# Reordering the projections, the key copies and the exponentials of a hybrid attention/recurrence layer

## The chip, the core and the metric

The program runs on one core of one Trainium2 chip. The metric is the device time of one execution, in microseconds (us): lower is better. Names of engines below: PE is the matrix engine (matmuls and transposes), PEld its weight loads, DVE the vector engine, ACT the scalar engine, POOL the general engine, and SP the queue from which all transfers of this kernel are issued. Each of them has its own list of instructions, written in the order of the source; semaphores hold an instruction until what it needs is there, and what stands behind it on its list waits too.

## What is computed

One decoder layer over 1024 tokens of width 1024, in float32. After an RMSNorm, one projection feeds two mixers: dilated sliding-window attention with 8 heads of 64, and a gated linear recurrence (HGRN2) with 4 heads of 128. Their outputs are joined and projected, and a squared-ReLU MLP of width 4096 follows. The part that matters here, cut down from the reference:

```python
q_a, k_a, v_a, q_h, f_h, i_h, g_h = jnp.split(h @ w_in[layer], splits, axis=-1)
for window, dilation in ((128, 1), (512, 4), (2048, 16)):
    s = einsum(q, k) * 64 ** -0.5 + alibi_bias          # causal, keys by stride
    m = max(s);  p = exp(s - m);  den = sum(p);  o = p @ v / den
attn = sum_i softmax_i(m_i + log den_i) * o_i           # three patterns joined per position
rec  = hgrn2_recurrence(q_h, f_h, i_h, g_h, ...)
x = x + rmsnorm(concat[rmsnorm(attn), rec] @ w_out)
x = x + rmsnorm(relu(rmsnorm(x) @ w_ff1) ** 2 @ w_ff2)
```

## The kernel before

**Split numbers.** Each float32 matrix is kept as two halves, a rounded high part and the remainder. `split_into` makes them: ACT copies the high part (L85), DVE subtracts it (L86). A projection is a chain of `three_pass` steps of three matmuls (L89, L90, L91), high by high, low by high, high by low.

**Stages.** The recurrence heads come first, one after the other (`hgrn_core`). While one runs, PE is kept busy with the projections of the next. In the last of them (h = 3) the projections of the attention pairs 0 and 1 begin. Then comes the attention loop of 64 steps; the out-projection and the MLP follow, and the change does not touch their code.

**The attention loop.** Eight heads in four pairs. A head has eight steps, `ITEMS`: D0 to D3 (the first four blocks of queries, densely), F0 and F1 (far keys, four classes of stride), N0 and N1 (near keys of the last four blocks). Step s is item s % 8 of head s // 8, and a pair takes 16 steps. Inside a step these helpers are called, and their order in the source is the order on each engine:

- `raise_` takes the exponentials of the *next* step's scores on ACT (L883; a D item has one, F and N items have two), which need the negative row maximum in `stat`. For F and N that maximum is joined over the patterns by `joint` (L869, L870 on DVE), from a small matmul `px` (`swap_max`, L864).
- `look` makes scores for a later step: matmuls with the key halves `kh` and `kl` into a bank `ps` (L828, L829), then bias and maximum on DVE (L833).
- `turn` transposes this step's exponentials on PE (`pt_D` L893, `pt_N` L902, `pt_F` L905), then copies the high half on ACT (L915, L917, L922) and subtracts on DVE (L918, L920, L923).
- `weigh` multiplies a turned item by the values, one step later (`pov`, `pov_far`; L939, L951, L957). `finish` turns the result back (L977), adds on DVE (L981) and divides on POOL (L982).
- `fill` takes projection steps from a list of generators, `queue`, and puts them between these. A unit is one `three_pass`, three matmuls. `UNITS` says how many units a step gets, half ahead of `weigh` and half at the end of the step; steps without an entry ask for a time instead (`fill(500.0)`).

**The projections of a pair** (`attn_proj`, six half projections of eight units). Queries, both halves (`pm_aq`); then values, both halves (`pm_av`); then keys, both halves (`pm_ak`). A half of the values is scaled on DVE (L746, tile `vf`), transposed on PE (`pvt`, L729), copied on ACT (L732) and subtracted on DVE (L733). A half of the keys is read from its bank on DVE (L677, tile `kf`), copied into `kh` twice on ACT (L688, 64 partitions each), subtracted into `kl` twice on POOL (L689), and four transfers bring each half to the other 64 partitions (L692, L693). The second half of the keys goes on a list, `put_off`, and `keys_late` does all of its work at once: in step 13 of a pair's 16 steps, after `while not put_off: fill(1.0)` has put the rest of the key projection on PE in one go. Step 14 then makes the first scores of the next pair from these keys. Pair `pr + 2` enters the queue in step 14 of pair `pr`.

**The last pair.** Heads 6 and 7 have no projections of attention left beside them. PE is filled with the recurrent half of the out-projection of the first four row blocks (`early_out`, tile `pwe`, 32 units). Its left operands are the rows `erows`, multiplied by a gain on POOL (`row_rec`, L1026), turned on PE (`pmt`, L1066) and split on ACT and DVE into `emt`. The table `hooks` names the steps in which these and the splits of the weights (`w_get`, tiles `wh`, `wl`, `woh`, `wol`) are done.

Of the kernel before, what the change touches and what calls it, by code (L numbers as in the profile page):

```python
# [17 lines left out]
P = 128  # L18
# [19 lines left out]
def hymba_layer(ctx, tc, x, w_in, w_out, w_ff1, w_ff2, g_pre, lb_logits, g_mix, g_post,  # L38
# [414 lines left out]
    def hgrn_core(h, scale, after=None):  # L453
# [128 lines left out]
        if h == HH - 1:  # L582
            while not put_off:
                fill(1.0)
            keys_late()
# [21 lines left out]
        fill(1500 * scale)  # L607
        for n in range(NT):
            V.scalar_tensor_tensor(gate[:, n], pos[n // 4][:, n % 4], rs[:, n:n + 1], gate[:, n],
                                   op0=ALU.mult, op1=ALU.mult)  # L610
# [61 lines left out]
    put_off = []  # L672

    def keys_read(pr, pm, hf):
# [4 lines left out]
        return full  # L679

    def keys_off(pr, stacks, full, hf):

        def place_of(t):
            return t.rearrange("p (r m) -> p r m", r=DIL)[:, :, hf * P:(hf + 1) * P]
        src = full.rearrange("p (r m) -> p r m", r=DIL)
        for i, (a, b) in enumerate(halves):
            kh, kl = (place_of(stacks[i][n])[a:b] for n in ("kh", "kl"))
            S.activation(kh, src[a:b], AF.Copy)  # L688
            G.tensor_tensor(out=kl, in0=src[a:b], in1=f32(kh), op=ALU.subtract)  # L689
        for n in ("kh", "kl"):  # L690
            k0, k1 = (place_of(f32(stacks[i][n])) for i in range(2))
            nc.sync.dma_start(out=k0[64:128], in_=k0[0:64])  # L692
            nc.sync.dma_start(out=k1[0:64], in_=k1[64:128])  # L693

    def keys_late():
        while put_off:
            pr, stacks, src, hf, read = put_off.pop()
            keys_off(pr, stacks, src if read else keys_read(pr, src, hf), hf)

    def attn_proj(pr):  # L700
        stacks = [{}, {}]
        box = [None]
        w = w_get(A0 + 3 * pr, 0)
        for hf in range(2):
            sl = slice(hf * 512, hf * 512 + 512)
            for n, cost in enumerate(proj_t(w, f"aq{pr}", hf, box)):
                if hf == 0 and n == 4:
                    w_get(A0 + 3 * pr)
                yield cost
# [12 lines left out]
        w = w_get(A0 + 3 * pr + 1, 0)  # L722
        vs = slab("V8", f"v{pr}", F32R, (P, NT, 2, 2, 64))
        late = None

        def v_turn(full, hf):
            pt = bank("mm", f"pvt{pr}{hf}")
            for j in range(4):
                TE.transpose(pt[:, j * P:(j + 1) * P], full[:, j * P:(j + 1) * P], ident)  # L729
            ptv = pt.rearrange("p (j h d) -> p j h d", j=4, h=2)  # L730
            dst = vs[:, hf * 4:hf * 4 + 4]
            S.activation(dst[:, :, :, 0, :], ptv, AF.Copy)  # L732
            V.tensor_tensor(out=dst[:, :, :, 1, :], in0=ptv, in1=f32(dst[:, :, :, 0, :]), op=ALU.subtract)  # L733
        for hf in range(2):
            sl = slice(hf * 512, hf * 512 + 512)
            n = 0
            for cost in proj_t(w, f"av{pr}", hf, box):
                n += 1
                if n == 4 and late is not None:
                    v_turn(*late)  # L740
                    cost += 450.0
                if n == 5 and hf == 0:
                    w_get(A0 + 3 * pr + 1)
                yield cost
            full = half(f"vf{pr}{hf}")
            V.tensor_tensor(out=by_class(full), in0=in_blocks(box[0]), in1=in_blocks(rrow[:, sl]), op=ALU.mult)  # L746
            late = (full, hf)
            yield 650.0
        while pr > 0 and not first_done[pr - 1]:
            yield None  # L750
        w = w_get(A0 + 3 * pr + 2, 0)
        for i in range(2):
            stacks[i]["kh"] = slab("S", f"kh{pr}_{i}", F32R)
            stacks[i]["kl"] = slab("S", f"kl{pr}_{i}", F32R)
        for hf in range(2):
            sl = slice(hf * 512, hf * 512 + 512)
            n = 0
            for cost in proj_t(w, f"ak{pr}", hf, box):
                n += 1
                if n == 3 and hf == 0:  # L760
                    v_turn(*late)
                    cost += 450.0
                if n == 6 and hf == 0:
                    for r in range(DIL):
                        nc.sync.dma_start(out=v_dram[pr][r].rearrange("(n i) c -> i n c", i=32),
                                          in_=f32(vs[32 * r:32 * r + 32]).rearrange("p n h a d -> p n (h a d)"))
                    if pr == 0:
                        far_load(0)
                if n == 6 and hf == 0:
                    w_get(A0 + 3 * pr + 2)  # L770
                yield cost
            if hf == 0 and pr == AH // 2 - 1:
                early_rows()
            if hf == 0:
                keys_off(pr, stacks, keys_read(pr, box[0], hf), hf)
            else:
                put_off.append((pr, stacks, box[0], hf, False))
            pairs[pr] = (stacks, vs)
            yield 650.0

# [91 lines left out]
    def raise_(hd, kind, g):  # L872
# [9 lines left out]
        for pe, i in jobs:  # L882
# [305 lines left out]
    def open_attention():  # L1188
# [3 lines left out]
        look(0, "N", 0)  # L1192

    for h in range(HH):
# [9 lines left out]
        43: lambda: row_rec(0),  # L1204
        44: lambda: w_get(WO0, 0),
        45: lambda: [drain(), row_turn(0, 0, tag="mm"), w_get(WO0 + 1, 0), row_rec(1)],
# [984 lines left out]
```

## Time and profile before

| | before |
|---|---|
| median of 3 runs | 1235.7 us (1234.51 to 1236.78) |
| the profiled execution: time / span of its profile | 1235.14 us / 1233.0 us |
| PE busy | 1209.1 us, 98% of the span |
| DVE / ACT / POOL busy | 862.0 / 546.4 / 322.4 us |
| mean granted PE clock over the span | 0.993 |
| transfers | 174.21 MB, mean 141 GB/s |

The span runs from the first to the last instruction; 2.1 us of the profiled time lie outside it. Busy time of PE includes matmuls that overlap their neighbours' ends, so 98% says that PE had something in hand, not that it ran at its best. The granted clock is the share of full speed that PE was given. A trace has each instruction's start and length and, in square brackets, how long its engine sat idle before it and what ended that. The recurrence ends at about 302 us, the attention loop runs from there to about 540 us, and the rest is the out-projection and the MLP.

### The profile page before, as it was taken

How to read it: one execution, taken by the hardware profiler on the slowest of the kernel's cores; microseconds unless marked ns; L12 is line 12 of the kernel's file. 1: busy time of each engine (PE TensorE's matmuls, PEld its weight loads, DVE VectorE, ACT ScalarE, POOL GpSimd, SP SyncE). 2: the span in 40 equal slices, each digit the busy share in tenths (PEclk: the TensorE clock that was granted, in tenths of full speed). 3: DMA queues.
4: the chain of work that ended last, by engine and by line, in shares of the span. 5: the costliest groups of instructions: out<-in, count | busy, mean ns of one | idle time of the engine just before them, and what ended most of it. 6: DMA issues, size and time to landing. Idle time of an engine off the chain costs nothing.

```text
span 1233.0 us, 17255 instructions
## 1 busy us (share of the span) xinstructions
PE 1209.1 (98%) x6350; PEld 1032.7 (84%) x6350; DVE 862.0 (70%) x1478; ACT 546.4 (44%) x1067; POOL 322.4 (26%) x321
## 2 busy tenths in 40 slices
PE   9999999999999999999999999999999999999998
PEld 8898989888878787878888888888888888888886
DVE  5697979786656556758679666576669655388796
ACT  7633324223555556666565222222235353434462
POOL 0110101012112123146150676756632000000022
PEclk9999999999999998999999999999999999999999
DMA  5231413125252527354333546455487634433337
GB/s 215 69 91 56 120 56 107 35 80 149 64 132 81 140 72 185 95 191 137 115 137 126 190 170 231 173 186 179 143 308 283 239 98 159 154 98 91 120 101 274
DMA packets 86483, 174.21 MB, mean 141 GB/s; under 512 B 12160, under 2 KB 38784, under 8 KB 86400
## 3 DMA queue, kind: packets, MB, share of 16 engines
q1 hardware_dynamic: 86400, 173.12, 43.2%
q8 instruction: 50, 0.82, 0.3%
q14 instruction: 33, 0.27, 0.1%
HBM read 117.76 MB, written 49.04 MB: 135 GB/s over the span
## 4 chain that ended last, share of the span: by engine, by line
PE 90%; ACT 3%; DVE 3%; issue 1%; DMA 1%; SPq 0%; POOL 0%; DVEq 0%; POOLq 0%; ACTq 0%
PE f L1931 18%; PE f2s L1931 7%; PE pig L91 2%; PE pig L89 2%; PE pig L90 2%; PE pl L480 2%; PE pwo L90 2%; PE pwo L91 2%; PE pwo L89 2%; PE pm_av L89 1%; PE pm_f L89 1%; PE pm_f L91 1%; PE pm_av L91 1%; PE pm_f L90 1%; PE pm_av L90 1%
## 5 line engine op out<-in xcount | busy, mean ns | idle before, releaser
L86 DVE TENSOR_TENSOR al<-ar,ah 128x1024 fp32r<-128x1024 f32 x56 | 70.6, 1261 | 80.2 <-ACT ah L85 77.8
L1931 PE MATMUL f<-bh,ah 128*128 128x512 f32 x320 | 124.5, 389 | 0.0
L1931 PE MATMUL f<-bl,ah 128*128 128x512 f32 x320 | 124.5, 389 | 0.0
L1931 PE MATMUL f<-bh,al 128*128 128x512 f32 x320 | 124.5, 389 | 0.0
L85 ACT ACTIVATE ah<-ar 128x1024 fp32r<-128x1024 f32 x56 | 59.2, 1057 | 90.1 <-DMA ar<-actd 85.9
L1931 PEld LDWEIGHTS f<-bh,ah 128*128 128x128 f32 x320 | 60.1, 188 | 12.6
L1931 PEld LDWEIGHTS f<-bl,ah 128*128 128x128 f32 x320 | 60.1, 188 | 12.5
L1931 PEld LDWEIGHTS f<-bh,al 128*128 128x128 f32 x320 | 60.1, 188 | 12.4
L2005 POOL TENSOR_SCALAR lbl<-ssq 128x1 f32<-128x1 f32 x4 | 3.3, 821 | 244.3 <-ACT fd L2001 244.2
L1554 POOL TENSOR_TENSOR e<-x,e 128x512 f32<-128x512 f32 x14 | 21.6, 1540 | 132.4 <-DVE x L1505 132.4
L1931 PE MATMUL f2s<-bh,al 128*128 128x512 f32 (+1 forms) x128 | 48.9, 382 | 0.0
L1931 PE MATMUL f2s<-bl,ah 128*128 128x512 f32 (+1 forms) x128 | 48.9, 382 | 0.0
L1931 PE MATMUL f2s<-bh,ah 128*128 128x512 f32 (+1 forms) x128 | 48.9, 382 | 0.0
L982 POOL TENSOR_TENSOR anat<-anat,stat 128x128 f32<-128x128 f32 (+1 forms) x24 | 13.1, 544 | 124.8 <-DVE anat L981 120.7
L86 DVE TENSOR_TENSOR bl<-br,bh 128x1024 fp32r<-128x1024 f32 x32 | 40.1, 1253 | 0.9 <-ACT bh L85 0.8
L664 POOL COPY tout<-traw 128x256 f32<-128x256 f32 x16 | 11.8, 736 | 107.3 <-DMA traw<-in_bias_tab_dram 73.7
L1948 ACT ACTIVATE acc<-f 128x512 f32<-128x512 f32 x28 | 16.8, 598 | 45.9 <-PE f L1931 45.8
L86 DVE TENSOR_TENSOR wl<-raw,wh 128x1024 fp32r<-128x1024 f32 x23 | 29.1, 1267 | 10.3 <-ACT wh L85 10.2
L85 ACT ACTIVATE bh<-br 128x1024 fp32r<-128x1024 f32 x32 | 33.6, 1050 | 3.9 <-PE f L1931 2.8
L689 POOL TENSOR_TENSOR kl<-kf,kh 64x512 fp32r<-64x512 f32 x16 | 20.5, 1279 | 47.7 <-ACT kh L688 47.1
L89 PE MATMUL pwo<-woh,mt 128*128 128x512 f32 x80 | 31.7, 397 | 0.5 <-ACT esum L1089 0.5
L718 POOL TENSOR_TENSOR ql<-qf,q 64x512 fp32r<-64x512 f32 x16 | 21.4, 1336 | 40.3 <-ACT q L717 28.5
(1702 smaller groups left out, 4029.3 us busy)
## 6 DMA issues: line engine op xcount, KB each, us to landing
ar<-actd SPq DMA_DIRECT2D x56, 512.0 KB, 3.7
br<-in_w_ff_dram SPq DMA_DIRECT2D x16, 1024.0 KB, 6.1
w1r<-in_w_ff_dram SPq DMA_DIRECT2D x14, 1024.0 KB, 6.5
raw<-in_w_in_dram SPq DMA_DIRECT2D x26, 512.0 KB, 3.8
actd<-e SPq DMA_DIRECT2D x17, 768.0 KB, 4.2
actd<-e SPq DMA_DIRECT2D x11, 1024.0 KB, 4.1
vd<-v SPq DMA_DIRECT2D x16, 256.0 KB, 3.8
raw<-in_w_out_dram SPq DMA_DIRECT2D x8, 512.0 KB, 4.2
```

Source lines behind the costliest of these rows:

```text
L85: S.activation(hi, src, AF.Copy)
L86: eng.tensor_tensor(out=lo, in0=src, in1=f32(hi), op=ALU.subtract)
L89: TE.matmul(dst, lhs[0], rhs[0], start=start, stop=False)
L90: TE.matmul(dst, lhs[0], rhs[1], start=False, stop=False)
L91: TE.matmul(dst, lhs[1], rhs[0], start=False, stop=stop)
L480: TE.matmul(pl[:, n % 2, :192], kt[:, n * P:(n + 1) * P], sets[u // 2][:, n % 4], start=True, stop=True)
L689: G.tensor_tensor(out=kl, in0=src[a:b], in1=f32(kh), op=ALU.subtract)
L718: G.tensor_tensor(out=lo[a:b], in0=full[a:b], in1=f32(stacks[i]["q"][a:b, sl]), op=ALU.subtract)
L982: G.tensor_tensor(out=dst, in0=dst, in1=st["rd"][:, b].unsqueeze(2).to_broadcast([P, n, 64]), op=ALU.mult)
L1554: eng[0].tensor_tensor(out=e1[:, 3], in0=a21, in1=e1[:, 2], op=ALU.add)
L1931: TE.matmul(pm, a[:, j, c], b[:, j, d], start=start and j == 0 and q == 0, stop=stop and j == 1 and q == 2, skip_group_check=True)
L1948: S.activation(acc_at(p, i), pm, AF.Copy)
```

## The change

Six things are done together; the arithmetic and the number of instructions of each kind stay.

1. A pair projects its queries, then the first half of its values, then both halves of its keys, then the second half of its values. The turning of a half of the values (`values_turn`) is taken out of its fixed place and done in a later projection.
2. The key work is cut into four jobs for each pair (one for each head of the pair and each half): one ACT copy, one POOL subtraction, two transfers. `key_job` does one job per step, in steps 1, 2, 3, 6 and 7 of a head. (Pair 0 does its jobs at once.)
3. Of the two exponentials of an F or N item the second stands behind `turn` in the step, not ahead of it.
4. `joint` for the near items comes one step earlier (4, not 5); `far_queries` comes earlier in its step; the first near scores of head 0 stand behind one more fill.
5. All four pairs stand in the queue from the start; a pair waits for `second_done` of the pair two before it. `UNITS` has four rows, and every step of the loop is filled by it.
6. `hooks` does the preparation of the early out-projection one to two steps later: the first row's gain in step 45 (43 before), the first row turn in 47 (45), the second in 50 (49), the third in 52 (51).

```diff
@@ hgrn_core
         if h == HH - 1:
-            while not put_off:
+            while keys_done[0] < 2:
                 fill(1.0)
-            keys_late()
...
         fill(1500 * scale)
+        if h == HH - 1:
+            look(0, "N", 0)
@@ keys
+        key_jobs.extend((pr, i, hf, full) for i in range(2))
+        keys_done[pr] += 1
...
+    def key_job():
+        if not key_jobs:
+            return
+        pr, i, hf, full = key_jobs.pop(0)
+        a, b = halves[i]
...
+        S.activation(kh[a:b], src, AF.Copy)
+        G.tensor_tensor(out=kl[a:b], in0=src, in1=f32(kh[a:b]), op=ALU.subtract)
+        c, d = halves[1 - i]
+        for t in (kh, kl):
+            nc.sync.dma_start(out=f32(t[c:d]), in_=f32(t[a:b]))
+
+    def values_turn():
+        pr, vs, full, hf = turn_later.pop(0)
+        pt = bank("mm", f"pvt{pr}{hf}")
...
@@ attn_proj
+        while pr > 1 and not second_done[pr - 2]:
+            yield None
...
+                if hf == 0 and n == 2 and turn_later:
+                    values_turn()
...
+        def values(hf):
+            for n, cost in enumerate(proj_t(wv, f"av{pr}", hf, box)):
+                if n == 4:
+                    w_get(A0 + 3 * pr + 1 + hf)
+                yield cost
...
+        yield from values(0)
         while pr > 0 and not first_done[pr - 1]:
             yield None
...
+            keys_read(pr, box[0], hf)
             if hf == 0 and pr == AH // 2 - 1:
                 early_rows()
...
+        yield from values(1)
@@ the loop
-    UNITS = ((2, 3, 4, 3, 2, 2, 2, 2), (3, 3, 4, 4, 3, 2, 2, 2), (4, 4, 4, 4, 3, 3, 3, 3))
+    UNITS = ((2, 3, 3, 4, 3, 3, 3, 3), (3, 3, 3, 4, 2, 3, 3, 2), (3, 3, 3, 4, 2, 3, 3, 2), (2,) * 8)
...
+    queue += [attn_proj(2), attn_proj(3)]
...
-        if i in (3, 5):
-            joint(hd, int(i == 5))
-        raise_(*((hd, *ITEMS[i + 1]) if i < 7 else (hd + 1, *ITEMS[0])))
-        if s % 16 == 13 and s < n_steps - 16:
-            while not put_off:
+        if i in (3, 4):
+            joint(hd, int(i == 4))
+        coming = (hd, *ITEMS[i + 1]) if i < 7 else (hd + 1, *ITEMS[0])
+        raise_(*coming, which=(0,))
+        if s % 16 in (11, 13) and s < n_steps - 16:
+            while keys_done[s // 16 + 1] < (1 if s % 16 == 11 else 2):
                 fill(1.0)
...
         turn(hd, kind, g)
+        raise_(*coming, which=(1,))
...
-        if s % 16 == 13 and s < n_steps - 16:
-            keys_late()
+        if i in (1, 2, 3, 6, 7):
+            key_job()
+        if s == 47:
+            drain()
+            values_turn()
+            early_sums()
+            queue.extend(early_out(t) for t in range(NE))
```

**What moves on PE at the border from pair 0 to pair 1** (last items of head 1, first scores of head 2). In a name such as `pt1_F1` the first digit is the head; in `pm_ak11` the digits are the pair and the half; the number behind the last underscore is a buffer. Line numbers of the changed kernel are a few higher. Before:

```order
L91 MATMUL pm_ak11_3607<-hTh11_94,wl21_3297 128x512
L905 MATMUL pt1_F1_3662<-ident_77,pf1_3378 128x128 x3
L951 MATMUL pov1_far_3672<-ptFh1_3619,vf0_0_2949 128x128
...
L977 MATMUL pov1_1_3633<-ident_77,pd1_3377 128x128 x2
L828 MATMUL ps2_D0_3701<-kh1_0_3494,q1_0_3140 128x128
L829 MATMUL ps2_D0_3701<-kl1_0_3495,q1_0_3140 128x128
L902 MATMUL pt1_N0_3706<-ident_77,pn1_3436 128x128 x4
```

Now, with the units of the next pair's queries and the turned values of this pair between them:

```order
L91 MATMUL pm_aq20_3659<-hTh00_88,wl22_3615 128x512
L908 MATMUL pt1_F1_3664<-ident_77,pf1_3394 128x128 x3
L89 MATMUL pm_aq20_3659<-hTh00_88,wh22_3614 128x512
...
L980 MATMUL pov1_1_3644<-ident_77,pd1_3393 128x128 x2
...
L710 MATMUL pvt11_3693<-ident_77,vf11_3657 128x128 x4
...
L831 MATMUL ps2_D0_3713<-kh1_0_3341,q1_0_3132 128x128
L832 MATMUL ps2_D0_3713<-kl1_0_3342,q1_0_3132 128x128
L905 MATMUL pt1_N0_3718<-ident_77,pn1_3459 128x128 x4
```

Between the turn of F1 and the turn of N0 there stood no unit of projection; now three units and a turn of values stand there. Five units of keys (15 matmuls in a row) stood right ahead of the turn of F1 before; the last key matmul now stands 44 rows ahead of it.

**What moves on ACT at the same place.** Before, the two exponentials of N0 (`pn1`, x2), the turned copies of F1, the two key copies, and the two exponentials of N1 follow one another:

```order
L883 ACTIVATE pn1_3436,stat1_3376<-pn1_3436,stat1_3376 128x256 x2
L915 ACTIVATE ptFh1_3619<-pt1_F1_3662 128x256
L917 ACTIVATE ptFh1_3619<-pt1_F1_3662 64x128 x2
L688 ACTIVATE kh1_0_3494<-kf11_3684 64x4x128
L688 ACTIVATE kh1_1_3496<-kf11_3684 64x4x128
L883 ACTIVATE pn1_3436,stat1_3376<-pn1_3436,stat1_3376 128x256 x2
L922 ACTIVATE ptNh1_3707<-pt1_N0_3706 128x4x128
```

Now:

```order
L886 ACTIVATE pn1_3459,stat1_3392<-pn1_3459,stat1_3392 128x256
L918 ACTIVATE ptFh1_3629<-pt1_F1_3664 128x256
L920 ACTIVATE ptFh1_3629<-pt1_F1_3664 64x128 x2
L886 ACTIVATE pn1_3459,stat1_3392<-pn1_3459,stat1_3392 128x256
L713 ACTIVATE v1_3262<-pvt11_3693 128x8x64
L886 ACTIVATE pn1_3459,stat1_3392<-pn1_3459,stat1_3392 128x256
L925 ACTIVATE ptNh1_3719<-pt1_N0_3718 128x4x128
L886 ACTIVATE pn1_3459,stat1_3392<-pn1_3459,stat1_3392 128x256
```

The key copies are gone from this place (the last of them stands seven rows ahead of the first exponential shown), a copy of turned values has come, and each item's second exponential stands behind the copies of the item before it.

**What moves on DVE in head 6**, in the last pair. `swap6_1` and `stat6` are the steps of `spread_max` and `joint`, `ptl6_2` the low halves of D2 and D3, `emt` the split of an early row. Before:

```order
L923 TENSOR_TENSOR ptl6_2_5194<-pt6_D2_5192,pth6_2_5193 128x3x128
L856 TENSOR_TENSOR swap6_1_5210<-stat6_5024,pick321_134 128x4x32
L869 TENSOR_TENSOR stat6_5024<-px6_0_5182,stat6_5024 128x4
L870 TENSOR_SCALAR stat6_5024<-stat6_5024 128x4
L923 TENSOR_TENSOR ptl6_2_5194<-pt6_D3_5221,pth6_2_5193 128x4x128
```

Now:

```order
L926 TENSOR_TENSOR ptl6_2_5178<-pt6_D2_5176,pth6_2_5177 128x3x128
L859 TENSOR_TENSOR swap6_1_5193<-stat6_4994,pick321_134 128x4x32
L86 TENSOR_TENSOR emt0_4778<-pmt1_0_5195,emt0_4778 128x512
L872 TENSOR_TENSOR stat6_4994<-px6_0_5166,stat6_4994 128x4
L873 TENSOR_SCALAR stat6_4994<-stat6_4994 128x4
L926 TENSOR_TENSOR ptl6_2_5178<-pt6_D3_5206,pth6_2_5177 128x4x128
```

The split of the second early row has come to stand ahead of the joined maximum, which the exponentials of F0 wait for.

More of the change, by code (lines that the diff above doesn't have):

```diff
@@ L881, in raise_ @@
             jobs = [(st["F"][:, r], 8 + r) for r in range(2 * g, 2 * g + 2)]
-        for pe, i in jobs:
+        for pe, i in (jobs[w] for w in which if w < len(jobs)):
             S.activation(pe, pe, AF.Exp, bias=st["nm"][:, i:i + 1], accum_out=st["dn"][:, i:i + 1])
@@ L1281, in hymba_layer @@
             look(hd + 1, "N", 0)
-        if s == 53:
+        if s == 54:
             row_turn(3, 0, tag="s")
```

136 lines of the change are left out of this document (50 added, 86 removed).

## The prediction

> **What bounds the kernel now.** I read the page first, then the busy time by stage, then PE's timeline where the stages lose time, then ACT and DVE at the same places.
>
> ```profile
> span 1233.0 us, 17255 instructions
> PE 1209.1 (98%) x6350; PEld 1032.7 (84%) x6350; DVE 862.0 (70%) x1478; ACT 546.4 (44%) x1067; POOL 322.4 (26%) x321
> ```
>
> PE bounds the whole; 23.9 us of its span are idle. The change adds and removes no matmul, so it can only win idle time, and time in which PE runs below its clock. The stages show where that is. Columns: window, its length, busy time (and count) of PE, PEld, DVE, ACT, POOL, then PE's granted clock.
>
> ```profile
> 296.00:544.00 248.00, 233.01 (x1369) 199.41 (x1368) 153.03 (x483) 148.79 (x396) 60.45 (x70) 0.97 0.41 110
> 300.00:304.00 4.00, 2.81 (x23) 2.54 (x22) 3.19 (x6) 0.65 (x2) 0.70 (x2) 1.00 0.60 140
> 352.00:364.00 12.00, 8.94 (x43) 7.03 (x42) 5.35 (x18) 6.37 (x20) 2.93 (x3) 0.86 0.42 97
> 416.00:428.00 12.00, 9.16 (x45) 7.51 (x44) 6.80 (x22) 5.75 (x15) 2.92 (x3) 0.86 0.45 115
> 476.00:488.00 12.00, 9.54 (x46) 8.12 (x45) 7.25 (x17) 8.53 (x22) 6.35 (x5) 0.72 0.52 124
> 492.00:504.00 12.00, 9.11 (x63) 7.89 (x62) 9.24 (x28) 8.22 (x24) 3.57 (x4) 1.00 0.72 215
> 524.00:544.00 20.00, 17.81 (x96) 13.77 (x95) 11.44 (x21) 14.98 (x42) 7.28 (x16) 1.00 0.36 98
> ```
>
> The attention loop holds 14.99 us of the idle time (248 less 233.01), and six stretches hold 14.63 of it: 1.19 at its start, 3.06, 2.84 and 2.46 at the three borders between pairs, 2.89 and 2.19 in the last pair. Only the borders also lose clock: 0.14 × 12 = 1.7 us twice and 0.28 × 12 = 3.4 us, 6.7 at most; some of it falls on idle time, so I count 6.0. The most there is to win is about 14.6 + 6 = 20.6 us.
>
> What PE waits for at the three borders, in brackets:
>
> ```profile
> 354.21 0.33 PE L951 MATMUL pov_far<-ptFl,vf 128*128 128x128 f32 x1 [0.59 <-DVE ptFl L918]
> 358.36 0.93 PE L902 MATMUL pt_N<-ident,pn 128*128 128x128 f32 x4 [2.12 <-ACT pn L883]
> ...
> 420.77 1.18 PE L902 MATMUL pt_N<-ident,pn 128*128 128x128 f32 x4 [2.12 <-ACT pn L883]
> ...
> 477.75 0.66 PE L1066 MATMUL pmt<-ident,erows 128*128 128x128 f32 x4 [1.21 <-POOL erows L1026]
> 479.17 0.45 PE L828 MATMUL ps_D<-kh,q 128*128 128x128 f32 x1 [0.76 <-DMA kh<-kh]
> 482.62 0.79 PE L89 MATMUL pwe<-wh,emt 128*128 128x512 f32 x1 [0.41 <-ACT emt L85]
> ```
>
> Why the exponentials are late at the first border, on DVE and then on ACT:
>
> ```profile
> 355.29 1.08 DVE L677 TENSOR_TENSOR kf<-pm_ak,rrow 128x512 f32<-128x512 f32 x1
> ...
> 356.40 1.28 ACT L688 ACTIVATE kh<-kf 64x512 fp32r<-64x512 f32 x2 [2.70 <-DVE kf L677]
> 357.70 0.51 ACT L883 ACTIVATE pn<-pn,stat 128x256 f32<-128x256 f32 x1
> ```
>
> The late half of the keys stands in the way: its reading (1.08), then its two copies (1.28), then the exponentials PE waits for. Nothing of the next pair could run on PE meanwhile, since the border's units had been spent ahead of it.
>
> **The change part by part.**
>
> *The borders.* Keys come before the second values, so their four jobs end two steps ahead of the border, one per step; the 1.08 + 1.28 leave the chain, and 3 units and a turn of values stand between the turns of F1 and N0 where none stood. From start to start a small product takes 0.12 us and a projection matmul 0.23, so a unit of three takes 0.7:
>
> ```profile
> 346.65 0.28 PE L939 MATMUL pov<-ptl,v 128*128 128x256 f32 x1
> 346.77 0.28 PE L939 MATMUL pov<-pth,v 128*128 128x256 f32 x1
> ...
> 447.21 0.48 PE L89 MATMUL pm_av<-hTh,wh 128*128 128x512 f32 x1
> 447.52 0.39 PE L90 MATMUL pm_av<-hTl,wh 128*128 128x512 f32 x1
> 447.75 0.39 PE L91 MATMUL pm_av<-hTh,wl 128*128 128x512 f32 x1
> ```
>
> From the turn of F1 to that of N0 PE now has three units (2.1), six far products (0.7), and ten more small ones (a finish, a turn of values, scores, 1.0), 3.8 us. ACT needs for N0 its first exponential (0.5), the copies of F1 (0.9) and the second exponential (0.5), 1.9 us. Late next is the split of the next queries' weights, now made in the second values' fifth unit and not in the keys:
>
> ```profile
> 352.89 0.36 ACT L915 ACTIVATE ptFh<-pt_F 128x256 fp32r<-128x256 f32 x1
> 353.15 0.55 ACT L917 ACTIVATE ptFh<-pt_F 64x128 fp32r<-64x128 f32 x2
> ...
> L86 DVE TENSOR_TENSOR wl<-raw,wh 128x1024 fp32r<-128x1024 f32 x23 | 29.1, 1267 | 10.3 <-ACT wh L85 10.2
> L85 ACT ACTIVATE bh<-br 128x1024 fp32r<-128x1024 f32 x32 | 33.6, 1050 | 3.9 <-PE f L1931 2.8
> ```
>
> About 3.6 us of PE lie ahead of its first use, against 1.05 (the copy, priced by one of the same shape) and 1.27, 2.3 us; if a second piece of that size is queued in front, it costs 0 to 1 us a border. I take 0. The key transfers were issued right before use; now eight of them lie two steps and more ahead. On SP they are passed by the values' spill and by weights that are used a pair later; the far values they feed are first read in the next pair's fifth step, so I count nothing. Borders one and two: 3.06 + 2.84 = 5.9 us won.
>
> At the third border the queue is empty in steps 46 and 47: a turn of values, then the turn of the first early row, then at once the unit that needs its split. The prices of a copy on ACT and of a subtraction on DVE, the same for both tiles, which have one shape:
>
> ```profile
> L732 ACT ACTIVATE v<-pvt x8: 597/597/600, 270.4 to 461.3; 128x512 fp32r<-128x512 f32 x8
> ...
> L86 DVE TENSOR_TENSOR emt<-pmt,emt x4: 680/686/691, 482.6 to 508.3; 128x512 fp32r<-128x512 f32 x4
> ```
>
> Both copies run on ACT behind the first turn: 1.2 us, with 0.45 of the second turn under it, 0.75 left. DVE ends its two subtractions at 0.6 + 0.69 + 0.69 = 1.98, when PE's third matmul would have started at 1.66: 0.3 more. So 2.46 becomes 1.1, and 1.35 are won. Its gain on POOL is done two steps ahead now. Borders together: 7.25 us, between 5 and 8.4.
>
> *The clock.* Within the loop it fell behind these three stretches only, and not behind 1.19, or behind 2.89 cut in three by work. The rows behind the first border show it: a matmul of a unit takes 0.63 there,
>
> ```profile
> 359.37 0.63 PE L90 MATMUL pm_aq<-hTl,wh 128*128 128x512 f32 x1
> ```
>
> against 0.39 at full clock. With idle of at most 1.1 left per border I take all 6.0 us as won. The Trainium skill ("TensorE: Matmul & The Clock Gate", section on HAM oscillation) gives the rule "no PE-idle gaps >~3.4µs". The longest gap here is 2.12 us and the clock fell all the same, so here the measurement decides; by that rule the stalls would not be the cause, and the sum would lack these 6.0.
>
> *The start.* The first near scores waited for a bank; now three units stand ahead of them.
>
> ```profile
> 304.01 0.36 PE L828 MATMUL ps_N<-kh,q 128*128 128x256 f32 x1 [1.20 <-issue]
> 308.94 0.40 PE L828 MATMUL ps_D<-kh,q 128*128 128x512 f32 x1
> ...
> 306.14 2.15 DVE L609 SCALAR_TENSOR_TENSOR gate<-po,hrs,gate 128x128 f32<-128x128 f32 x8
> 308.21 0.55 DVE L833 CUSTOM_DVE_ANT_0 pd<-ps_D,bt 128x384 f32<-128x384 f32 x1
> ```
>
> But the scores of D3 need the bank that DVE frees at about 308.7, behind the eight gates, and DVE's list is the same length as before. PE would reach D3 at 308.94 − 1.20 = 307.74 and wait 1.0. I count 0, between 0 and 1.2.
>
> *The last pair.* Its stalls at 494 to 502:
>
> ```profile
> 494.38 0.39 PE L864 MATMUL px<-pick,swap 128*128 128x4 f32 x2 [0.55 <-DVE stat L833]
> 495.51 0.36 PE L828 MATMUL ps_F<-kh,qc 128*128 128x192 f32 x1 [0.75 <-DVE stat L833]
> 501.88 0.55 PE L905 MATMUL pt_F<-ident,pf 128*128 128x128 f32 x3 [1.59 <-DVE ptl L923]
> ...
> 498.36 0.17 DVE L869 TENSOR_TENSOR stat<-px,stat 128x4 f32<-128x4 f32 x1
> 499.63 0.46 ACT L883 ACTIVATE pf<-pf,stat 128x192 f32<-128x192 f32 x1 [0.62 <-DVE stat L870]
> 500.53 0.57 ACT L922 ACTIVATE pth<-pt_D 128x512 fp32r<-128x512 f32 x1
> ```
>
> A weight split still stands on DVE ahead of D3's maximum; one unit more and one row turn less on PE cover 0.3 of the 1.30, 1.0 stays. For F0 the split of the second row is now ahead of `joint`: 0.60 + 0.69 + 2 × 0.17 + 0.45 + 0.57 + 0.45 = 3.1 us, against 1.5 us of PE (the turn of D3 0.45, finish 0.2, a unit 0.7, `px` 0.15): 1.6, as before. So 2.89 becomes 2.6; taken as 0, between −1 and +2. In the stretch to 544 the units lie one by one between the turns and not in fours; I take 0.5 of the 2.19, between 0 and 2.
>
> *Interleaving.* The first matmul after another kind of work takes 0.31 us to the next start where others take 0.23, 0.08 more. Counted over PE's order there are 7 runs more than before: +0.6 us.
>
> *Sum.* −7.25 − 6.0 − 0.5 + 0.6 = −13.1 us. The profiled execution took 1235.14, 0.6 below the median of 1235.7, so: 1222.0 from the one, 1222.6 from the median, which I give.
>
> **The rivals.**
>
> *The clock does not follow* (by that page's rule: the half clock is not these gaps' doing, or returns with the 1.6 us of the last pair). For it: the gaps are short. Against it: full clock in the windows with 1.19 and 2.89 idle. Then 1235.7 − 7.1 = 1228.6. Chance 0.10.
>
> *The next wait takes half of the borders:* the weights split late, or the turn of values, 1 us and more at each, and a part of the clock with it; 6 to 7 us are won, about 1229. For it: six more pieces on ACT and DVE near the border. Against: DVE is busy 5.35 and ACT 6.37 of 12 us there. Chance 0.08.
>
> *All of it goes,* the last pair too: 1235.7 − 14.6 − 6 + 0.6 = 1215.7. Against it: the chain to F0 above. Chance 0.08.
>
> *Slower: the second exponentials.* Each now waits for the turned copies of the item before: 0.57 before F0, 0.36 + 0.55 before F1 and N0, 0.60 before N1, 3 us a head and 24 us in eight heads, if PE has nothing to put there. It decides where PE has under about 1.5 us (the turn itself, the copy and the exponential) between two turns. With two units (1.4) and the products there are 1.8 at the thinnest place, before F0 of head 7, so it should bite there at most; if it bites everywhere, 1235.7 − 13.1 + 24 = 1246.6. Chance 0.10.
>
> *It does nothing* (the units run out early and the borders are bare as before): 1235 to 1236. Chance 0.03; the order shows units at all three.
>
> **How the numbers follow.** Forecast 0.61, 1218 to 1226 by the bounds above. The rivals at 1228.6 and 1229 carry it to 0.79 up to 1231, half of the complete one makes 0.83 from 1216. Measurements of this kernel can tell 0.2%, 2.5 us, from no change. Faster by more: 0.61 + 0.10 + 0.08 + 0.08 = 0.87; the same 0.03; slower 0.10.
>
> **What would show it.** Right: no wait of PE over 0.3 us at the first two borders, clock 1.00 in their windows, about 1.1 us idle at the third in front of `pwe`, 1 us at D3 of head 0, about 1.6 us at `pt_F` of head 6. Wrong: `pt_N` or `pt_F` waiting for ACT in most heads (the second exponentials); `pm_aq` waiting for `wh` or `wl` (the weights); a clock below 0.95 anywhere in the loop without such a stretch; or idle time in the loop that falls by less than 6 us.

## The result: faster by 6.3 us, less than half of what was forecast

The changed kernel takes 1229.42 us (median of 5 runs, 1228.77 to 1229.97) beside 1235.7 of the kernel before; the ratio is 0.9949, interval 0.9934 to 0.9963. The forecast was 1222.6, a gain of 13.1. So the sign held, and 6.8 us of the gain are missing: the time lies outside the forecast's own bounds of 1218 to 1226, and inside the wider range, up to 1231, only by the room that was given to rivals.

The page of the kernel after, span and busy time:

```profile
span 1226.8 us, 17215 instructions
PE 1205.5 (98%) x6350; PEld 1032.1 (84%) x6350; DVE 868.7 (71%) x1478; ACT 547.4 (45%) x1067; POOL 322.8 (26%) x321
```

To see in which stage the time was won, I split both traces where the first late unit of the out-projection (`pwo`) starts. Columns of the windows, here and below: window, length, then busy time (and count) of PE, PEld, DVE, ACT, POOL, PE's granted clock, share of the transfer engines, GB/s. Before:

```profile
296.00:538.37 242.37, 227.59 (x1344) 195.17 (x1342) 149.10 (x477) 145.53 (x389) 58.23 (x65) 0.97 0.41 108
538.37:1233.00 694.63, 688.57 (x3112) 571.24 (x3112) 489.23 (x510) 287.00 (x431) 230.14 (x211) 1.00 0.50 172
```

After:

```profile
296.00:532.80 236.80, 224.53 (x1349) 194.81 (x1348) 152.02 (x480) 145.88 (x388) 53.96 (x63) 0.97 0.43 117
532.80:1226.80 694.00, 688.11 (x3112) 571.45 (x3112) 489.05 (x510) 286.87 (x431) 230.35 (x211) 1.00 0.49 172
```

The tail is as long as it was (694.6 and 694.0). The loop is 5.6 us shorter, but PE's idle time in it has only gone from 14.8 to 12.3 us, and its clock is still 0.97. Yet the first two borders have gone as forecast. After, at the start, at borders one and two, and around the third border and the beginning of the last pair:

```profile
308.00:312.00 4.00, 2.92 (x16) 2.16 (x15) 3.90 (x18) 2.48 (x8) 1.49 (x2) 1.00 0.97 259
352.00:364.00 12.00, 12.00 (x77) 10.60 (x76) 8.18 (x24) 8.05 (x21) 2.20 (x3) 1.00 0.65 177
416.00:428.00 12.00, 12.00 (x75) 10.52 (x75) 8.36 (x34) 6.18 (x15) 3.20 (x3) 1.00 0.96 254
464.00:500.00 36.00, 26.94 (x139) 22.61 (x138) 20.14 (x60) 19.36 (x49) 8.58 (x8) 0.81 0.57 163
```

Borders one and two have no idle time left and full clock (before: 3.06 and 2.84 idle, 0.86). The start has 1.08 idle, at the place forecast. But the stretch from 464 to 500 holds 9.06 us of idle time and, at 0.81 of the clock over 36 us, 6.8 us of clock at most (some of it falls on idle time). What PE waits for there, from its timeline:

```profile
466.81 0.33 PE L960 MATMUL pov_far<-ptNl,v 128*128 128x128 f32 x1 [0.56 <-DVE ptNl L926]
...
469.38 0.47 PE L89 MATMUL pwe<-wh,emt 128*128 128x512 f32 x1 [1.07 <-DVE v L714]
...
474.34 0.50 PE L89 MATMUL pwe<-wh,emt 128*128 128x512 f32 x1 [1.17 <-ACT wh L85]
475.60 0.49 PE L90 MATMUL pwe<-wl,emt 128*128 128x512 f32 x1 [0.75 <-DVE wl L86]
...
482.02 0.50 PE L90 MATMUL pwe<-wol,emt 128*128 128x512 f32 x1 [1.61 <-DVE wol L86]
...
490.84 0.79 PE L89 MATMUL pwe<-woh,emt 128*128 128x512 f32 x1 [3.29 <-ACT woh L85]
492.19 0.80 PE L90 MATMUL pwe<-wol,emt 128*128 128x512 f32 x1 [0.56 <-DVE wol L86]
```

The first two belong to the third border. The second stands where a wait was forecast (1.07; forecast 1.1), but by the trace what ends it is the subtraction of the turned values (`v`, L714), not the row's split from which the forecast had worked it out, so the closeness is in part luck. The five others, 7.4 us, all stand in front of a unit of the early out-projection whose weights are just being split. Each split is a copy on ACT and a subtraction on DVE, which the units then read. ACT at the last two splits:

```profile
477.49 1.05 ACT L85 ACTIVATE woh<-raw 128x1024 fp32r<-128x1024 f32 x1
...
483.89 0.49 ACT L925 ACTIVATE pth<-pt_D 128x384 fp32r<-128x384 f32 x1 [4.65 <-PE pt_D L896]
...
489.74 1.04 ACT L85 ACTIVATE woh<-raw 128x1024 fp32r<-128x1024 f32 x1
```

This is a ring. PE reaches the unit right behind the split in the source and stands; the transposes behind the unit on PE's list (`pt_D`) come late, so ACT stands for them (4.65 us at 483.89, in 1.61 of which PE stands itself) and gets to its next exponentials and its next split late, for which PE stands again. DVE has the subtraction at the end of it, 1.2 to 1.3 us:

```profile
480.75 1.22 DVE L86 TENSOR_TENSOR wol<-raw,woh 128x1024 fp32r<-128x1024 f32 x1
...
490.82 1.31 DVE L86 TENSOR_TENSOR wol<-raw,woh 128x1024 fp32r<-128x1024 f32 x1 [0.30 <-ACT woh L85]
```

The guard in `early_out` (`while j >= done[1] - WO0`) asks only that the split has been *issued*. In the kernel before, `hooks` splits these three weights in steps 45, 47 and 48, and among PE's waits there is none of `pwe` for one of them; the change splits them in steps 48, 49 and 51, two and three steps later and not one to two, and its units, two in every step, arrive while the split is being made.

### The profile page after: what moved, and what is told of

It reads as the page before. It is cut to its first block, busy times and chain, and to the rows that moved or that the text cites. A ratio compares the mean times of both kernels' runs of the same rounds, so it can differ in the third digit from the quotient of the medians.

```text
span 1226.8 us, 17215 instructions
## 1 busy us (share of the span) xinstructions
PE 1205.5 (98%) x6350; PEld 1032.1 (84%) x6350; DVE 868.7 (71%) x1478; ACT 547.4 (45%) x1067; POOL 322.8 (26%) x321
## 4 chain that ended last, share of the span: by engine, by line
PE 94%; DVE 2%; ACT 2%; issue 1%; DMA 1%; SPq 0%; POOL 0%; DVEq 0%; POOLq 0%; ACTq 0%
PE f L1931 18%; PE f2s L1931 7%; PE pig L91 2%; PE pig L89 2%; PE pig L90 2%; PE pl L480 2%; PE pwo L89 2%; PE pwo L91 2%; PE pwo L90 2%; PE pm_f L89 1%; PE pm_f L91 1%; PE pm_f L90 1%; PE pm_ak L89 1%; PE pm_aq L89 1%; PE pm_aq L91 1%; PE pm_aq L90 1%
## 5 line engine op out<-in xcount | busy, mean ns | idle before, releaser
L1931 PEld LDWEIGHTS f<-bl,ah 128*128 128x128 f32 x320 | 60.1, 188 | 12.3
```

The lines of the kernel that those rows point to most:

```text
L1931: TE.matmul(pm, a[:, j, c], b[:, j, d], start=start and j == 0 and q == 0, stop=stop and j == 1 and q == 2, skip_group_check=True)
```

## The experiments

All times are medians; the kernel before took 1235.66, 1235.44 and 1236.16 us in the three groups of runs, and each ratio is to the runs of its own group.

**Late weights: four kernels on the changed kernel.** The theories were: W, the late splits of the output weights; J, the second row's turn, now ahead of `joint`; and the two other parts of the change that could have cost or won time, the second exponentials and the spread key jobs.

The splits put earlier, nothing else:

```diff
-        46: lambda: row_rec(1),
-        47: lambda: row_turn(0, 0, tag="mm"),
-        48: lambda: w_get(WO0 + 1, 0),
-        49: lambda: [w_get(WO0 + 2, 0), load_bias(AH - 1), row_rec(2)],
+        46: lambda: [w_get(WO0 + 1, 0), row_rec(1)],
+        47: lambda: [row_turn(0, 0, tag="mm"), w_get(WO0 + 2, 0)],
+        48: lambda: w_get(WO0 + 3, 0),
+        49: lambda: [load_bias(AH - 1), row_rec(2)],
...
-        51: lambda: w_get(WO0 + 3, 0),
```

> The changed kernel with the splits of the out-projection weights 1, 2 and 3 moved from steps 48, 49, 51 to steps 46, 47, 48, ahead of the units that read them; nothing else. Theory W (the last pair lost its time because PE reached units whose weights ACT and DVE had not split yet, and the transposes behind them on PE then held ACT up, which held the next split): the waits of the early out-projection on wh, wl, woh, wol, 7.4 us in the changed kernel, fall below 1 us, the half clock between 476 and 500 us goes, and the time falls from 1229.4 to 1217 to 1221. Theory J (the split of the second early row, which stands ahead of the joined maximum, is the cause; the weights are only late because of it): the waits move to the turn of F0 of head 6 and at most 3 us are won, 1226 to 1229. Theory C (the even two units per step are too few, or the clock is lost for itself): no change, 1229.

Measured: 1219.27 us (1218.81 to 1220.12), ratio 0.9867 (0.9851 to 0.9884); 10.2 us below the changed kernel. Its windows:

```profile
464.00:500.00 36.00, 32.42 (x205) 28.21 (x204) 25.65 (x80) 25.23 (x65) 9.02 (x9) 0.95 0.62 181
476.00:488.00 12.00, 11.45 (x72) 9.68 (x71) 9.30 (x33) 8.35 (x24) 3.56 (x4) 1.00 0.81 228
488.00:496.00 8.00, 8.00 (x58) 7.21 (x57) 3.96 (x13) 5.75 (x19) 0.40 (x1) 1.00 0.58 190
```

From 464 to 500 the idle time falls from 9.06 to 3.58 us and the clock's loss from 6.8 to 1.8 (0.05 × 36): 5.5 + 5.0 = 10.5 at most, against 10.2 by the medians. Theory W stands, and it prices the error.

The second row's turn back in step 49:

```diff
-        49: lambda: [w_get(WO0 + 2, 0), load_bias(AH - 1), row_rec(2)],
-        50: lambda: [row_turn(1, 0), row_rec(3)],
+        49: lambda: [row_turn(1, 0), w_get(WO0 + 2, 0), load_bias(AH - 1), row_rec(2)],
+        50: lambda: row_rec(3),
```

> The changed kernel with the turn of the second early row put back from step 50 to step 49, so that its split no longer stands between the scores of F1 and the joined maximum; the weights as late as before. Theory J: 4 us or more are won, 1222 to 1225, and the weights' waits shrink with it. Theory W: the weights are late all the same, within 2 us of 1229.4, with 3 us and more of waits for woh left.

Measured: 1229.35 us (1226.54 to 1230.7), ratio 0.9946 (0.9930 to 0.9961), the same as the changed kernel. The timeline shows the wait of 3.29 gone and shorter ones in its place; the waits on the last two splits sum to 5.7 us, against 5.5 in the changed kernel:

```profile
482.24 0.50 PE L89 MATMUL pwe<-woh,emt 128*128 128x512 f32 x1 [1.63 <-ACT woh L85]
...
484.34 0.50 PE L90 MATMUL pwe<-wol,emt 128*128 128x512 f32 x1 [1.60 <-DVE wol L86]
...
491.07 0.50 PE L89 MATMUL pwe<-woh,emt 128*128 128x512 f32 x1 [1.64 <-ACT woh L85]
492.38 0.52 PE L90 MATMUL pwe<-wol,emt 128*128 128x512 f32 x1 [0.80 <-DVE wol L86]
```

J falls: without the row turn ahead of it PE waits for the same splits.

Both exponentials ahead of the turn again:

```diff
-        raise_(*coming, which=(0,))
+        raise_(*coming)
...
-        raise_(*coming, which=(1,))
```

> The changed kernel with both exponentials of a next item ahead of the turn again, as in the kernel before; all else as changed. If the second exponential behind the turned copies costs PE time, as the rival in the prediction had it, this is faster, by up to 24 us if everywhere, by 1 us if only in the last pair. If it helps (the turned copies and what PE does with them come 0.5 us earlier), this is slower by 1 to 4 us. By the prediction's view (covered on both sides) the first 45 steps show no difference: the turn of N1 of head 5 starts within 0.5 us of the changed kernel's 465.3.

Measured: 1230.56 us (1229.39 to 1232.1), ratio 0.9959 (0.9944 to 0.9974): 1.1 above the changed kernel, within what can be told. The forecast's slower rival falls: the second exponential behind the turned copy costs nothing, and may win 1.

Both key jobs of a half at once, in all pairs:

```diff
-        if pr == 0:
-            key_job()
-            key_job()
+        key_job()
+        key_job()
```

> The changed kernel with both jobs of a half of the keys done right after it is read, for every pair, and not one per step. If the gain at the borders comes from where the keys stand among the projections, this stays within 1.5 us of 1229.4 and the windows of the first two borders show no idle time and a full clock. If it comes from spreading the copies one per step, stalls of 1 us and more come back where the copies stand, and 2 to 6 us are lost.

Measured: 1230.47 us (1229.57 to 1233.9), ratio 0.9963 (0.9948 to 0.9978), 1.0 above the changed kernel: spreading the jobs over the steps is not where the gain comes from.

**Late weights, from the other side.** In the kernel before, only the splits moved to the steps of the change (WO1 to 48, WO2 to 49, WO3 to 51):

```diff
-        45: lambda: [drain(), row_turn(0, 0, tag="mm"), w_get(WO0 + 1, 0), row_rec(1)],
+        45: lambda: [drain(), row_turn(0, 0, tag="mm"), row_rec(1)],
...
-        47: lambda: w_get(WO0 + 2, 0),
-        48: lambda: w_get(WO0 + 3, 0),
-        49: lambda: [row_turn(1, 0), row_rec(2), load_bias(AH - 1)],
+        48: lambda: w_get(WO0 + 1, 0),
+        49: lambda: [row_turn(1, 0), w_get(WO0 + 2, 0), load_bias(AH - 1), row_rec(2)],
...
-        51: lambda: row_turn(2, 0),
+        51: lambda: [row_turn(2, 0), w_get(WO0 + 3, 0)],
```

> The kernel before, with nothing changed but the steps of the output weights' splits: WO1 from step 45 to 48, WO2 from 47 to 49, WO3 from 48 to 51, as the change has them. Theory W (a weight split that stands in the same step as the units that read it stops TensorE in its order, the transposes behind the unit hold ScalarE, and ScalarE holds the next split): the last pair loses as in the changed kernel, 6 to 12 us, 1242 to 1248. Rival (the last pair is lost only by the denser filling of the change, two units in each of 16 steps; the splits alone would not matter at before's spacing of 500 to 540 ns): 1235 to 1238.

Measured: 1247.69 us (1245.27 to 1248.52), ratio 1.0092 (1.0077 to 1.0107), 12.3 us slower than before. Its summary of PE's waits has the same lines, and its last pair, below them, has 8.9 us of idle time and a clock of 0.76 between 488 and 524:

```profile
PE pwe L89 <- ACT woh L85: 3.5, 2, 1.9
PE pwe L90 <- DVE wol L86: 2.4, 2, 1.6
PE pwe L89 <- ACT wh L85: 2.2, 1, 2.2
...
488.00:524.00 36.00, 27.14 (x133) 22.76 (x133) 18.33 (x55) 17.08 (x46) 4.86 (x5) 0.76 0.39 128
```

In the kernel before, the same stretch has 2.9 and 1.00:

```profile
488.00:524.00 36.00, 33.11 (x222) 29.25 (x222) 25.97 (x94) 24.12 (x67) 4.98 (x7) 1.00 0.41 116
```

So the late splits cost 10 to 12 us in either kernel, with either filling.

**The unit held back instead of the split put earlier.** The changed kernel with a guard that asks for a split issued in an earlier step:

```diff
-            while j >= done[1] - WO0:
+            while j >= old_split[0]:
...
         hd, i = divmod(s, 8)
+        old_split[0] = done[1] - WO0
...
```

> The changed kernel with the splits left at steps 48, 49 and 51, but a unit of early output may only be placed when the split of its weights was issued in an earlier step. Theory W: what costs is TensorE standing in its order behind a split that isn't done; with the units held back a step the waits on woh, wol, wh and wl between 470 and 495 go, and the units that are left over run later, where they cover other waits: 1219 to 1223. Rival (the last pair is short of filling work as long as the weights come late, so holding the units back only turns waits on weights into waits on exponentials): 1226 to 1231.

Measured: 1224.36 us (1223.35 to 1226.83), ratio 0.9913 (0.9897 to 0.9930). Half of the loss comes back, 5.1 of 10.2 us; neither range held it. The waits on the splits are shorter and not gone: a split issued one step ahead, behind the other work of ACT and DVE, is still not always done, as two of them show:

```profile
475.76 0.50 PE L90 MATMUL pwe<-wl,emt 128*128 128x512 f32 x1 [0.77 <-DVE wl L86]
...
486.75 0.79 PE L90 MATMUL pwe<-wol,emt 128*128 128x512 f32 x1 [0.68 <-DVE wol L86]
```

**What won the borders: keys first, or filling?** The forecast named both. With the splits early, four kernels make a table: the keys ahead of the second half of the values or last (as before), and the filling of the change or that of before. All four do the key jobs at once (by the code, spread jobs would hold buffers that the next projection needs when the keys are last; no run tries it). The keys ahead, the new filling (one edit against the kernel with the early splits, that of the key jobs above):

> The kernel with the three splits at steps 46, 47 and 48 (1219.3), and both key jobs of a half done at once after it is read instead of one in a step. If spreading the jobs is worth nothing beside the place of the keys among the projections, as with the late weights: 1219 to 1222. If the late weights hid its worth: 1224 and more.

Measured: 1220.61 us (1219.59 to 1220.82), ratio 0.9875 (0.9860 to 0.9889). The keys last:

```diff
+                if n == 3 and hf == 1:
+                    values_turn()
...
         yield from values(0)
+        yield from values(1)
...
             keys_read(pr, box[0], hf)
...
-        yield from values(1)
...
```

> As the kernel with the splits at 46, 47 and 48 and the key jobs at once, with the order of the projections put back: queries, both halves of the values, keys (the first half of the values is turned inside the second, the second inside the keys, as before). Theory O (the borders' gain of 12 to 13 us comes from the keys standing ahead of the second half of the values, so that they are done long before the border): the idle time and the half clock at the borders come back, 1229 to 1234 beside 1219 to 1222 with the keys ahead. Rival (the borders gained from the even filling and from the query copies moved up, and the order is free): within 2 us of the kernel with the keys ahead.

Measured: 1222.96 us (1222.48 to 1223.74), ratio 0.9896 (0.9881 to 0.9911). Theory O, my own, falls: beside the new filling the order of the projections is worth 2.4 us and not 10. The old filling, with the keys last:

```diff
-    queue += [attn_proj(2), attn_proj(3)]
...
-    UNITS = ((2, 3, 3, 4, 3, 3, 3, 3), (3, 3, 3, 4, 2, 3, 3, 2), ...
+    UNITS = ((2, 3, 4, 3, 2, 2, 2, 2), (3, 3, 4, 4, 3, 2, 2, 2), ...
...
+        if s % 16 == 14 and s // 16 + 2 < AH // 2:
+            drain()
+            queue.append(attn_proj(s // 16 + 2))
```

> As the kernel with the keys last (1223.0), with the old filling of the first two pairs too: the next pair's projections are queued at step 14 behind a drain, and the numbers of units a step are those of before. Theory F (what won the borders is that units of the next pair's queries are at hand in steps 13 to 15; the place of the keys is worth 2): the idle time and the half clock at borders one and two come back, 1230 to 1235. Rival (something else in the change won the borders, such as the second exponential): within 2 us of 1223.

Measured: 1233.58 us (1231.61 to 1234.56), ratio 0.9977 (0.9967 to 0.9986). And the old filling with the keys ahead (here with a `values_turn()` behind the drain):

> The same old filling, with the keys ahead of the second half of the values (beside 1220.6 with the new filling). Theory F: the borders are bare also with the keys ahead, 1228 to 1233. Rival, theory E (either of the two is enough: keys done early, or units at hand): 1220 to 1223. Rival, theory O (the keys alone): 1220 to 1223 as well, but then the kernel with both undone would have to lie far above the one with the keys last alone and this one not.

Measured: 1230.83 us (1230.13 to 1231.45), ratio 0.9955 (0.9940 to 0.9970).

| | new filling | old filling | difference |
|---|---|---|---|
| keys ahead | 1220.61 | 1230.83 | 10.2 |
| keys last | 1222.96 | 1233.58 | 10.6 |
| difference | 2.4 | 2.8 | |

By the times alone the two parts would add up: the filling 10.2 to 10.6 us, the place of the keys 2.4 to 2.8, for which the intervals overlap by a little. The traces do not bear that out, since the two differences of 10 us have different causes. With the keys last, the filling does what was forecast: the waits of the turn of N0 and N1 on the exponentials are 7.3 us in all with the old filling and 3.3 with the new, of which 2.35 stand at the third border. At the first border with the keys last, the copies of the late half stand in front of the exponentials as they did before, ACT first, then what PE does meanwhile, with the new filling:

```profile
352.30 1.28 ACT L699 ACTIVATE kh<-kf 64x512 fp32r<-64x512 f32 x2 [1.42 <-DVE kf L681]
353.61 0.51 ACT L890 ACTIVATE pn<-pn,stat 128x256 f32<-128x256 f32 x1
...
353.49 0.48 PE L89 MATMUL pm_aq<-hTh,wh 128*128 128x512 f32 x1
...
354.73 0.40 PE L91 MATMUL pm_aq<-hTh,wl 128*128 128x512 f32 x1
...
355.13 0.91 PE L909 MATMUL pt_N<-ident,pn 128*128 128x128 f32 x4
```

Two units of the next pair's queries run from 353.49 to 355.1, and the turn of N0 follows without a wait. With the old filling the same copies, and nothing to put there:

```profile
353.27 1.28 ACT L699 ACTIVATE kh<-kf 64x512 fp32r<-64x512 f32 x2 [2.99 <-DVE kf L681]
...
356.08 0.44 PE L909 MATMUL pt_N<-ident,pn 128*128 128x128 f32 x2 [2.34 <-ACT pn L890]
...
352.00:364.00 12.00, 9.66 (x58) 8.65 (x57) 6.29 (x21) 6.84 (x19) 2.92 (x3) 0.86 0.56 113
```

The wait of 2.34 and the clock of 0.86 are those of the kernel before (2.12 and 0.86). With the keys ahead, the old filling brings neither back:

```profile
PE pvt L709 <- DVE vf L757: 6.8, 4, 3.8
...
PE pt_N L904 <- ACT pn L885: 0.2, 1, 0.2
...
352.00:364.00 12.00, 10.54 (x68) 9.16 (x67) 8.10 (x25) 7.06 (x16) 0.40 (x1) 1.00 0.59 159
...
416.00:432.00 16.00, 16.00 (x99) 13.99 (x98) 10.81 (x40) 9.21 (x22) 3.19 (x3) 1.00 0.78 205
...
476.00:488.00 12.00, 8.88 (x39) 7.60 (x40) 7.91 (x23) 5.75 (x10) 0.00 (x0) 0.72 0.60 152
```

The turn of N0 and N1 waits 0.2 us in the whole run, and the clock is full at borders one and two. This kernel loses its time in front of the turn of the late values (`pvt`), which stands right behind their projection and waits for their scaling on DVE (`vf`): 1.46 us at the first border, 1.21 at the second, and 3.79 at the third. At the first two that place comes from the edit itself, which puts `values_turn` directly behind the drain; at the third the old filling has left the last units of the values right ahead of the turn. So the time is the one that theory F named, but its mechanism is not there, and for the wait on the exponentials at the first two borders theory E is the one that fits: either part alone takes most of it away (0.77 is left at the second border with the keys last and the new filling). What the old filling would cost with the keys ahead and the values turned later, no run shows. The two halves of the filling, the queue and `UNITS`, were not tried apart.

**Better versions.** The exponentials once more, with the splits early:

> The kernel with the splits at 46, 47 and 48 (1219.3), with both exponentials ahead of the turn again. If the second exponential behind the turned copy is worth nothing, 1219 to 1220.5; if it hides copies that would hold PE, as the forecast's rival had it the other way, 1221 to 1224; if it costs, below 1218.

Measured: 1220.56 us (1219.54 to 1221.42), ratio 0.9872 (0.9857 to 0.9887): 1.3 above the 1219.27 of the other group, the same 1 us as before and as little to be told.

With the splits early, one long wait is left at the third border, again in front of the first unit, and the clock is at 0.57 from 472 to 476, behind it. The releaser in brackets, an exponential, ends at 470.68; DVE's subtraction of the turned values ends at 470.64, and that is the one named in front of this unit in the changed kernel and in the one with both exponentials ahead (2.32). The high half of the first row, which the unit reads, was done at 469.33, so the row's split is not what ends the wait:

```profile
470.79 0.47 PE L89 MATMUL pwe<-wh,emt 128*128 128x512 f32 x1 [2.43 <-ACT pf L886]
...
468.00:472.00 4.00, 1.57 (x11) 1.08 (x10) 3.96 (x8) 2.77 (x6) 2.05 (x1) 1.00 0.77 205
472.00:476.00 4.00, 4.00 (x20) 3.61 (x19) 1.92 (x9) 1.72 (x3) 0.00 (x0) 0.57 0.89 227
```

The units queued a step later:

```diff
         if s == 47:
...
-            queue.extend(early_out(t) for t in range(NE))
...
-        48: lambda: w_get(WO0 + 3, 0),
+        48: lambda: [queue.extend(early_out(t) for t in range(NE)), w_get(WO0 + 3, 0)],
```

> The kernel with the splits at 46, 47 and 48, and the units of early output queued at step 48 instead of the end of step 47, so that the first of them no longer stands behind the first early row's turn (2.4 us idle there, and half clock in the window after it, some 4 us of clock and idle). Theory W: it gains 1 to 3 us, 1216 to 1218.5. Rival (step 47 is then bare, the idle time only takes another name): 1219 to 1221.

Measured: 1217.62 us (1217.45 to 1218.5), ratio 0.9850 (0.9834 to 0.9867), the best of all, 18.5 us below the kernel before; the 1.7 us to the version above are within what two groups of runs can tell. The rival's description is the one that the trace fits: the wait has taken another name, and the clock falls behind it as before.

```profile
472.96 0.58 PE L831 MATMUL ps_N<-kh,q 128*128 128x256 f32 x1 [2.22 <-DVE stat L836]
...
472.00:476.00 4.00, 3.04 (x9) 2.57 (x10) 3.48 (x15) 2.03 (x4) 0.00 (x0) 0.57 0.91 221
```

## Why the prediction was wrong in its size, point by point

- **The borders, −7.25: right at the first two, near at the third.** No idle time is left at the first two; from the turn of F1 to that of N0 PE takes 3.9 us at the first (forecast 3.8). The third has 0.56 + 1.07 = 1.6 (forecast 1.1), with another last cause than forecast. Of the two reasons given, units at the border and keys out of the chain, each takes away most of the wait on the exponentials by itself there, as the two kernels with one of them show; their prices do not simply add.
- **The clock, −6.0: right at borders one and two** (1.00 in both windows), and undone behind the third, where up to 6.8 us are lost. By the rule of the Trainium skill ("TensorE: Matmul & The Clock Gate", section on HAM oscillation), "no PE-idle gaps >~3.4µs", the clock would have stayed as it was. These runs speak against it once more, since full clock came back where gaps of 2.1 us were filled, and 0.57 follows single gaps of 2.43 and 2.22.
- **The start, 0: right.** The wait at D3 is 1.08 by the window, forecast 1.0.
- **The last pair, taken as 0, between −1 and +2: this is the step that failed.** I followed D3's maximum, `joint` and F0, and took "a weight split still stands on DVE ahead of D3's maximum" as the cost of moving the splits. The unit that reads the split, in the same step on PE's list, I did not follow. It costs 10.2 us (the splits put earlier) to 12.3 (the splits put late in the kernel before). The other direction of that term was mis-sized too: with the splits early the same work stands some 15 us earlier, and from 476 to 496 it has 0.55 us of idle time where it had 2.89 from 488 to 508. The turn of F0, for which I kept 1.6 us "as before", waits 0.2, so that chain does not bind. Those 2.3 us are the larger part of the 3.3 by which the version with the early splits wins more than 13.1 (16.4); the rest of that sum is not closed.
- **The stretch to 544, −0.5, and the interleaving, +0.6: neither came.** The same stretch, 5.6 us earlier in the changed kernel, has 2.1 us of idle time, and 2.19 before. In the loop PE's busy time fell by 3.1 us (227.59 to 224.53) at the same mean clock of 0.97, where 0.6 more was forecast. No run shows why.
- **The rivals.** "The next wait takes half of the borders" gave about 1229, and 1229.4 came; but it had the split weights at each border and in front of `pm_aq`, where no wait of that kind is seen, so its number is luck. The mechanism was named, the place was not: it is the output weights in front of `pwe`. The slower rival, the second exponentials, is refuted twice (1230.56 and 1220.56 with both ahead, neither of them faster than with the second behind).
- **The signs to look for** did their work: "idle time in the loop that falls by less than 6 us" stood among those that would make it wrong, and it fell by 2.5.

## What to carry to other kernels

When work that makes an operand is moved later, look on the reader's engine for the first instruction that needs it: a guard that asks only whether the producer has been issued lets filling work stop an engine that runs in order, and everything behind it. Filling between dependent steps has to be at hand at the seam itself, so queue the next stage's work ahead of the seam and not in it; with the keys last that was worth 10.6 us here. When two runs differ by the same time, compare their waits before you call it the same effect. After such a repair, look at the same place again: the last wait of 2.2 to 2.4 us only changed its name.

## What the runs showed of the chip that I had not expected

The clock answers late, and to short waits. In the changed kernel PE's clock is 0.59 in the four microseconds after the waits at 474 and 475, in which PE is busy throughout, and 0.50 in those after the 3.29 wait:

```profile
476.00:480.00 4.00, 4.00 (x18) 3.53 (x16) 1.97 (x10) 2.03 (x4) 0.00 (x0) 0.59 0.75 229
...
488.00:492.00 4.00, 0.79 (x1) 0.29 (x1) 2.57 (x7) 2.41 (x6) 0.40 (x1) 0.80 0.02 6
492.00:496.00 4.00, 3.81 (x13) 3.34 (x14) 1.14 (x5) 2.49 (x9) 0.00 (x0) 0.50 0.68 236
```

In the kernel with the early splits one wait of 2.43 us was followed by 0.57, while the 1.08 us at the start of the loop cost no clock in any run that has it, and neither did 1.59 us in the kernel before, at 501.88:

```profile
504.00:508.00 4.00, 4.00 (x30) 3.62 (x29) 1.92 (x8) 3.06 (x10) 0.00 (x0) 1.00 0.31 90
```

So a single wait of 2.43 us cost another 0.43 × 4 = 1.7 us in clock, and the 2.12 us at the first border before cost as much (0.14 × 12). The limit for a single wait lies between 1.6 and 2.1 us in these runs. Several short ones can add up, as 1.17 and 0.75 did ahead of the 0.59; how, these runs do not tell.
